# A decoder layer on one core: the output projection by seven half products for each pair of row tiles, its first products and the gate's sums inside the stage before it

## The chip, the cores and the metric

The kernel runs on one core of one Trainium2 chip. TensorE (PE) multiplies, VectorE (DVE), ScalarE (ACT) and GpSimd (POOL) work on elements, and the queue of SyncE (SP) issues nearly all transfers. The metric is the device time of one execution in microseconds (us); lower is better.

## The reference, cut to what matters

One layer with two parallel mixers (sparse attention "A", sliding-window attention "B"). The change is in what follows the attention, for 1024 positions and D = 1024:

```python
y_a = (merge_heads(o_a) * silu(z_a)) @ w_o_nsa        # (1024,512) @ (512,1024)
y_b = (merge_heads(o_b) * silu(z_b)) @ w_o_swa
m_a, m_b = split(merge)                                # columns of the input projection
y = (sigmoid(m_a) * y_a + sigmoid(m_b) * y_b) @ w_out  # (1024,1024) @ (1024,1024)
return x + gate * rms_norm(y, g_post)                  # gate = c @ w_ada[:, 2D:] + b_ada
```

## The kernel before, in words

All products are done in float32r with each operand split into a high part (a cast, on ACT) and a low part (operand minus high part, on POOL or DVE). One product of two splits is three matmuls: high by high, high by low, low by high. A matmul here takes a 128x128 block as weights and streams 512 columns.

After the attention come two stages. The **gated stage** (function `gated`) makes the gated sum `ym`, transposed (channels on partitions), in 16 steps: eight for mixer B (m = 0 to 7), then eight for mixer A. A step loads one block of `w_o` (through `wraw`, split into `wh` and `wl`, six buffers each), makes two half products of 12 matmuls (24 a step), and for each half DVE multiplies the PSUM bank by the merge gate (in `t2`, four buffers, loaded from DRAM and put through a sigmoid); in the A steps DVE also adds that to `ym` and splits `ym` into `ymh` and `yml`. Beside the B steps run `heads_out` (loads the heads' outputs `od`, splits them into `oh` and `ol`) and `w_out_block` (loads and splits `w_out`, into the places of the dead `hh` and `hl`). The **output stage** then has, for each of eight row tiles (128 positions) and each half of the columns, 24 matmuls into one bank (`out_products`), and `out_rows` makes the norm, gate and residual from the two banks and stores. Two row tiles of products are issued ahead; then `gate_rows` spreads the gate `amod` over a row by two plain float32 matmuls. The eight sums that give the gate (a multiply and reduce of 1024 elements, L1133) and their loads stand between the stages in the program.

PSUM has eight banks. `anybank` hands them out in a fixed cycle of eight, so the n-th call takes the bank of call n-8, and the matmul that starts in it waits until the readers of that one are done:

```python
order = ["s", "pt", "pj", "s", "pv", "pt", "s", "pj"]
cyc[0] += 1
return bank(order[cyc[0] % 8])
```

Each engine works its instructions in a fixed order that a scheduler sets when the kernel is built, and SP its transfers: what waits holds up all that is behind it. A tile's buffer is used again when its readers are done.

Of the kernel before, what the change touches and what calls it, by code (L numbers as in the profile page):

```python
# [14 lines left out]
P = 128  # L15
# [53 lines left out]
def hybrid_kernel(tc, io, out):  # L69
# [964 lines left out]
    with tc.tile_pool(name="ot", bufs=1, reuse_waits="tile") as op:  # L1034
        oh = [op.tile([P, S], F32R, name=f"oh{k}", tag=f"oh{k}") for k in range(8)]
        ol = [op.tile([P, S], F32R, name=f"ol{k}", tag=f"ol{k}") for k in range(8)]
        ym = {}
# [4 lines left out]
        def heads_out(k):  # L1042
            for half in range(2):
# [19 lines left out]
        for n, name in enumerate(MERGE[:KEEP]):  # L1063
            sg = op.tile([P, S], F32, name="sgm", tag=f"ym{7 - n}")
# [23 lines left out]
        woh, wol = [], []  # L1088
        ymh, yml = [], []

        def w_out_block(k):

            a, b = [], []
            for n in range(2):
                ns = slice(n * HS, n * HS + HS)
                raw = wp.tile([P, HS], F32, name="wraw", tag="wraw", bufs=3)
                nc.sync.dma_start(raw, io["w_out"][k * P : (k + 1) * P, ns])
                a.append(main.tile([P, HS], F32R, name=f"woh{k}", tag=f"hh{k}_{n}"))
                b.append(main.tile([P, HS], F32R, name=f"wol{k}", tag=f"hl{k}_{n}"))
                nc.scalar.copy(a[n], raw)  # L1100
                nc.gpsimd.tensor_tensor(b[n], raw, a[n].bitcast(F32), ALU.subtract)
            woh.append(a)
            wol.append(b)

        for m in range(8):
            ym[m] = op.tile([P, S], F32, name=f"ym{m}", tag=f"ym{m}")
            gated(m, "B", 1, lambda sl, ty, sg: nc.vector.tensor_tensor(ym[m][:, sl], ty, sg, ALU.mult))
            if m % 2:
                heads_out(m // 2)
            w_out_block(m)  # L1110
        for m in range(8):

            def emit(sl, ty, sg):
                nc.vector.tensor_tensor(sg, ty, sg, ALU.mult)
                nc.vector.tensor_tensor(ym[m][:, sl], ym[m][:, sl], sg, ALU.add)

            gated(m, "A", 0, emit)

            places = [(f"oh{m + 4}", f"ol{m + 4}")] * 4 + [("ym0", "ym1"), ("ym2", "ym3"), ("ym4", "ym5"), ("oh0", "ol0")]
            ymh.append(op.tile([P, S], F32R, name=f"ymh{m}", tag=places[m][0]))  # L1120
            yml.append(op.tile([P, S], F32R, name=f"yml{m}", tag=places[m][1]))
# [5 lines left out]
        cb2 = op.tile([P, D], F32, name="cb2", tag="ym6")  # L1127
        nc.sync.dma_start(cb2, io["c"].partition_broadcast(P))
        for k, place in enumerate(("ym7", "oh1", "ol1", "oh2", "ol2", "oh3", "ol3", "oh1")):
            blk = 16 + k  # L1130
            wa = op.tile([P, D], F32, name="wa", tag=place)
            nc.sync.dma_start(wa, io["w_adaT"][blk * P : (blk + 1) * P, :])
            nc.vector.tensor_tensor_reduce(  # L1133
                out=wa, in0=wa, in1=cb2, scale=1.0, scalar=smalls[:, 8 + blk : 9 + blk],
# [138 lines left out]
```

## Time and profile before

| what | value |
|---|---|
| time, median of 3 runs | 901.26 us (901.21 to 901.35) |
| time of the profiled execution | 900.77 us |
| its span, first to last instruction | 899.0 us |
| PE busy | 888.9 us, 99% of the span |
| DVE, ACT, POOL busy | 538.2, 505.6, 356.9 us |
| matmuls | 4538 |

The span is what the trace covers; 1.77 us of the profiled execution lie around it. A matmul's busy time includes its way through the array, so matmuls overlap and their pitch is read from their starts.

### The profile page before, as it was taken

How to read it: one execution, taken by the hardware profiler on the slowest of the kernel's cores; microseconds unless marked ns; L12 is line 12 of the kernel's file. 1: busy time of each engine (PE TensorE's matmuls, PEld its weight loads, DVE VectorE, ACT ScalarE, POOL GpSimd, SP SyncE). 2: the span in 40 equal slices, each digit the busy share in tenths (PEclk: the TensorE clock that was granted, in tenths of full speed). 3: DMA queues.
4: the chain of work that ended last, by engine and by line, in shares of the span. 5: the costliest groups of instructions: out<-in, count | busy, mean ns of one | idle time of the engine just before them, and what ended most of it. 6: DMA issues, size and time to landing. Idle time of an engine off the chain costs nothing.

```text
span 899.0 us, 14304 instructions
## 1 busy us (share of the span) xinstructions
PE 888.9 (99%) x4538; PEld 753.0 (84%) x4538; DVE 538.2 (60%) x1511; ACT 505.6 (56%) x1150; POOL 356.9 (40%) x428
## 2 busy tenths in 40 slices
PE   8999999999999999999999999999999999999997
PEld 7989888888888888888888888888887888887885
DVE  5866863465578677575585677566463372677322
ACT  6477732466676877565666777565464555442111
POOL 1000421365576866452544576453351366200000
PEclk7999999999999999999999999999999999999999
DMA  9873442342234332111222131211212677335432
GB/s 353 281 249 101 141 163 78 118 136 97 82 101 116 115 87 73 48 54 53 71 63 80 60 89 59 80 51 36 83 39 68 207 250 230 115 112 188 138 104 80
DMA packets 67087, 104.51 MB, mean 116 GB/s; under 512 B 8002, under 2 KB 25794, under 8 KB 67011
## 3 DMA queue, kind: packets, MB, share of 16 engines
q1 hardware_dynamic: 65856, 102.36, 35.1%
q10 hardware_dynamic: 1154, 1.23, 0.5%
q8 instruction: 36, 0.59, 0.3%
q14 instruction: 41, 0.33, 0.1%
HBM read 79.97 MB, written 19.92 MB: 111 GB/s over the span
## 4 chain that ended last, share of the span: by engine, by line
PE 95%; DVE 1%; DMA 1%; ACT 1%; issue 0%; POOL 0%; SPq 0%; DVEq 0%; POOLq 0%; ACTq 0%
PE b_pt L858 8%; PE b_pj L917 7%; PE b_pj L921 7%; PE b_pj L922 7%; PE b_pj L194 5%; PE b_pj L195 5%; PE b_pj L187 5%; PE b_s L790 5%; PE b_s L787 4%; PE b_pv L869 4%; PE b_pv L866 4%; PE b_s L1158 1%; PE b_s L1157 1%; PE b_s L1156 1%; PE b_s L1078 1%; PE b_s L1080 1%
## 5 line engine op out<-in xcount | busy, mean ns | idle before, releaser
L164 POOL TENSOR_TENSOR wl<-wraw,wh 128x512 fp32r<-128x512 f32 x102 | 133.7, 1313 | 137.7 <-ACT wh L161 86.6
L865 DVE TENSOR_TENSOR pl<-b_pt,ph 128x512 fp32r<-128x512 f32 x162 | 110.4, 687 | 63.2 <-ACT ph L864 62.3
L864 ACT CAST ph<-b_pt 128x512 fp32r<-128x512 f32 x162 | 93.8, 583 | 64.7 <-PE b_pt L858 51.2
L917 PE MATMUL b_pj<-hh,wh 128*128 128x512 f32 x288 | 117.6, 412 | 0.0
L922 PE MATMUL b_pj<-hh,wl 128*128 128x512 f32 x288 | 114.0, 396 | 0.0
L921 PE MATMUL b_pj<-hl,wh 128*128 128x512 f32 x288 | 113.1, 394 | 0.0
L821 POOL TENSOR_SCALAR ps<-ps,rr,gates 128x128 f32<-128x128 f32 (+7 forms) x64 | 52.7, 827 | 92.4 <-DVE rr L813 51.4
L194 PE MATMUL b_pj<-hl,wh 128*128 128x512 f32 x224 | 88.2, 394 | 0.0
L187 PE MATMUL b_pj<-hh,wh 128*128 128x512 f32 x224 | 88.0, 393 | 0.0
L195 PE MATMUL b_pj<-hh,wl 128*128 128x512 f32 x224 | 87.9, 393 | 0.0
L787 PE MATMUL b_s<-kh,q 128*128 128x256 f32 (+6 forms) x272 | 85.8, 323 | 0.0
L790 PE MATMUL b_s<-kl,q 128*128 128x256 f32 (+6 forms) x272 | 83.9, 316 | 0.0
L809 ACT ACTIVATE ps<-ps,mins 128x256 f32<-128x256 f32 (+7 forms) x96 | 64.9, 677 | 32.2 <-DVE mins L797 30.4
L161 ACT CAST wh<-wraw 128x512 fp32r<-128x512 f32 x94 | 57.5, 615 | 32.8 <-PE b_pj L194 11.7
L809 ACT ACTIVATE pw<-pw,mins 128x256 f32<-128x256 f32 (+4 forms) x96 | 60.7, 633 | 26.6 <-DVE mins L797 26.2
L869 PE MATMUL b_pv<-pl,V 128*128 128x512 f32 x162 | 67.5, 417 | 0.2
L866 PE MATMUL b_pv<-ph,V 128*128 128x512 f32 x162 | 65.3, 403 | 0.0
L922 PEld LDWEIGHTS b_pj<-hh,wl 128*128 128x128 f32 x288 | 54.1, 188 | 10.8
L921 PEld LDWEIGHTS b_pj<-hl,wh 128*128 128x128 f32 x288 | 54.4, 189 | 8.5
L880 POOL TENSOR_TENSOR ot<-ot,zt 64x512 f32<-64x512 f32 x32 | 41.2, 1288 | 49.9 <-DVE ot L879 41.0
L821 POOL TENSOR_SCALAR pw<-pw,rr,gates 128x640 f32<-128x640 f32 (+4 forms) x64 | 47.6, 748 | 32.4 <-DVE rr L813 18.0
L917 PEld LDWEIGHTS b_pj<-hh,wh 128*128 128x128 f32 x288 | 53.9, 189 | 7.5
(309 smaller groups left out, 2137.7 us busy)
## 6 DMA issues: line engine op xcount, KB each, us to landing
wraw<-in_w_blk SPq DMA_DIRECT2D x90, 256.0 KB, 2.9
wa<-in_w_adaT SPq DMA_DIRECT2D x23, 512.0 KB, 5.2
w1raw<-in_w SPq DMA_DIRECT2D x16, 256.0 KB, 3.4
od<-ot SPq DMA_DIRECT2D x64, 64.0 KB, 2.1
sp_MA<-sp SPq DMA_DIRECT2D x16, 256.0 KB, 2.0
wraw<-in_w_o SPq DMA_DIRECT2D x16, 256.0 KB, 3.4
wraw<-in_w_out SPq DMA_DIRECT2D x16, 256.0 KB, 3.7
t<-od SPq DMA_DIRECT2D x16, 256.0 KB, 4.0
```

The source lines that it names most:

```text
L164: chain("wl", nc.gpsimd.tensor_tensor(wl, raw, wh.bitcast(F32), ALU.subtract))
L187: ins = nc.tensor.matmul(t, lhsT=wh, rhs=hh[kc][half], start=(kc == 0), stop=False)
L194: nc.tensor.matmul(t, lhsT=wh, rhs=hl[kc][half], start=False, stop=False)
L195: nc.tensor.matmul(t, lhsT=wl, rhs=hh[kc][half], start=False, stop=(kc == KC - 1))
L787: ins = nc.tensor.matmul(sp[:, :n_in], lhsT=q, rhs=rh, start=True, stop=False)
L790: nc.tensor.matmul(sp[:, :n_in], lhsT=q, rhs=rl, start=False, stop=True)
L809: nc.scalar.activation(rows[r][:, :off], rows[r][:, :off], AF.Exp, scale=-1.0, bias=last_min[:, r : r + 1], accum_out=sums[:, r : r + 1])
L865: nc.vector.tensor_tensor(pl, t, ph.bitcast(F32), ALU.subtract)
L869: nc.tensor.matmul(pv, lhsT=v, rhs=pl, start=False, stop=(last and n == len(todo) - 1))
L917: ins = nc.tensor.matmul(self.t, lhsT=wh, rhs=hh[kc][self.half], start=(kc == 0), stop=False)
L921: nc.tensor.matmul(self.t, lhsT=wh, rhs=hl[kc][self.half], start=False, stop=False)
L922: ins = nc.tensor.matmul(self.t, lhsT=wl, rhs=hh[kc][self.half], start=False, stop=(kc == KC - 1))
```

## The change

The last product is done on 2 x 2 blocks. A11, A12, A21, A22 are 128 positions by 512 channels (row tiles p and p+4 of the gated sum; the second index is the half of the channels), and B11 to B22 the quarters of `w_out`. For each of four pairs p, seven products of 12 matmuls (128x512 by 512x512) take the place of eight. Their right sides are B11, B22, B21 and T1 to T4 (sums of the quarters), their left sides A11, A12, A22 and S1 to S4. The sums T are formed during the gated stage: `sums_b` in the B steps, `sums_a` in the A steps, from `w_out` rows that are loaded twice; B21 is loaded a third time (`last_set`). The sums S and the splits of the left sides (`row_set`) are made up to five products ahead. DVE adds the products up in SBUF. The gate's sums are cut into 16 of 512 elements, one in each step of the gated stage, all through one buffer (`wag`, of tag `xr`). In the list below "..." leaves out lines; T1, T2, T3, T4 are `B12-B11`, `B22-(B12-B11)`, `B22-B12` and `B21-T2`.

```diff
+        def sums_b(m):
+            k = m // 2
+            if m % 2 == 0:
+                rows[k] = w_rows(k), w_rows(k + 4)
+                r0, r1 = rows[k]
+                w_set("B11", k, r0[:, lo_], of_h(0, k))
+                nc.vector.tensor_tensor(r0[:, hi_], r0[:, hi_], r0[:, lo_], ALU.subtract)
+                w_set("T1", k, r0[:, hi_], of_h(1, k))
...
+        def sums_a(m):
...
+                r0, r1 = rows.pop(k)
+                nc.vector.tensor_tensor(r1[:, lo_], r1[:, lo_], r0[:, lo_], ALU.subtract)
+                nc.vector.tensor_tensor(r1[:, lo_], r1[:, lo_], r0[:, hi_], ALU.subtract)
+                w_set("T4", k, r1[:, lo_], of_heads(f"ol{k + 4}"))
...
+        wag = tmp("xr", 3)
+        def gate_load(k, n):
+            nc.sync.dma_start(wag, io["w_adaT"][(16 + k) * P : (17 + k) * P, n * HS : n * HS + HS])
...
-            w_out_block(m)
+            sums_b(m)
+            gate_sum(m, 0)
...
-            for half in range(2):
-                sl = slice(half * HS, half * HS + HS)
-                nc.scalar.copy(ymh[m][:, sl], ym[m][:, sl])
-                nc.vector.tensor_tensor(yml[m][:, sl], ym[m][:, sl], ymh[m][:, sl].bitcast(F32), ALU.subtract)
...
+        def split_rows(src, eng):
+            a = wp.tile([P, 4, P], F32R, name="wh", tag="wh", bufs=WBUFS)
+            b = wp.tile([P, 4, P], F32R, name="wl", tag="wl", bufs=WBUFS)
+            chain("high", nc.scalar.copy(a, src))
+            chain("vector" if eng is nc.vector else "pool", eng.tensor_tensor(b, src, a.bitcast(F32), ALU.subtract))
+            return a, b
...
+        def product(t, a, name):
+            for k in range(4):
+                bh, bl = W[name, k]
+                ins = nc.tensor.matmul(t, lhsT=a[0][:, k, :], rhs=bh, start=(k == 0), stop=False)
...
+                nc.tensor.matmul(t, lhsT=a[0][:, k, :], rhs=bl, start=False, stop=False)
+            for k in range(4):
+                nc.tensor.matmul(t, lhsT=a[1][:, k, :], rhs=W[name, k][0], start=False, stop=(k == 3))
...
+        STEPS = [("A11", "B11"), ("S3", "T3"), ("S1", "T1"), ("S2", "T2"), ("A22", "T4"), ("S4", "B22"), ("A12", "B21")]
+        todo = [(p, *f) for p in range(4) for f in STEPS]
+        todo.insert(2, todo.pop(7))
...
+            gate_load(m, 1)
+            gated(m, "A", 0, emit)
+            sums_a(m)
+            gate_sum(m, 1)
+            if m > 4:
+                sets_to(m - 4)
...
+        for step, (p, n, wn) in enumerate(todo):
+            sets_to(step + 5)
+            X, Y, V, Z = spare[p % 2]
+            t = anybank()
+            product(t, ready.pop((p, n)), wn)
+            if n == "A11":
+                nc.scalar.copy(X, t)
+            elif n in ("S3", "S1"):
+                held3[n] = t
+            elif n == "S2":
+                s3, s1 = held3.pop("S3"), held3.pop("S1")
+                nc.vector.tensor_tensor(Y, X, t, ALU.add)
+                nc.vector.tensor_tensor(Z, Y, s3, ALU.add)
+                nc.vector.tensor_tensor(V, Z, s1, ALU.add)
+                nc.vector.tensor_tensor(Y, Y, s1, ALU.add)
+            elif n == "A22":
+                nc.vector.tensor_tensor(Z, Z, t, ALU.add)
+                done_rows.append((p, [(1, V, V), (0, Z, Z)]))
+            elif n == "S4":
+                nc.vector.tensor_tensor(Y, Y, t, ALU.add)
+            elif n == "A12":
+                nc.vector.tensor_tensor(X, X, t, ALU.add)
+                done_rows.append((p + 4, [(1, Y, Y), (0, X, X)]))
+            if step == 3:
+                gate_rows()
```

The order of the products is thus A11 and S3 of pair 0, A11 of pair 1, then S1, (the two matmuls of `gate_rows`), S2, A22, S4, A12 of pair 0, S3 of pair 1 and so on.

Three places of the order that the engines work in (line numbers of the change are those of the changed kernel). The first is **POOL at the end of the gated stage**. Before, these are the last lows of `w_out` (L1101) and then only lows of `w_o` (L164), the last of them for steps A2 to A7:

```order
L1101 TENSOR_TENSOR wol6_8783<-wraw_8780,woh6_8782 128x512 [waits DMAHW5_49,Activation_49]
L164 TENSOR_TENSOR wl_8790<-wraw_8787,wh_8789 128x512 [waits DMAHW6_49,PE_49,Activation_49]
L1101 TENSOR_TENSOR wol7_8838<-wraw_8835,woh7_8837 128x512 [waits DMAHW0_49,Activation_49]
L1101 TENSOR_TENSOR wol7_8844<-wraw_8841,woh7_8843 128x512 [waits DMAHW2_49,Activation_49]
L164 TENSOR_TENSOR wl_8850<-wraw_8847,wh_8849 128x512 [waits DMAHW3_49,PE_49,Activation_49]
L164 TENSOR_TENSOR wl_8898<-wraw_8895,wh_8897 128x512 [waits DMAHW5_49,PE_49,Activation_49]
```

Now the lows of `w_o` for A6 (`wl_9166`) and A7 (`wl_9224`) stand there behind those of the first left sides (L1196: A11 of pair 0, then S3 of pair 0 from `t2_9214`); `wt` are T3 and T4:

```order
L1101 TENSOR_TENSOR wt_9154<-r_9102,wt_9154 128x512 [waits DMAHW7_49,Activation_49]
L1196 TENSOR_TENSOR wl_9159<-ym0_8395,wh_9158 128x512 [waits PE_49,Activation_49]
L164 TENSOR_TENSOR wl_9166<-wraw_9163,wh_9165 128x512 [waits PE_49,Activation_49]
L1101 TENSOR_TENSOR wt_9210<-r_9205,wt_9210 128x512 [waits DMAHW4_49,Activation_49]
L1101 TENSOR_TENSOR wt_9265<-r_9207,wt_9265 128x512 [waits DMAHW6_49,Activation_49]
L1196 TENSOR_TENSOR wl_9217<-t2_9214,wh_9216 128x512 [waits PE_49,Activation_49]
L164 TENSOR_TENSOR wl_9224<-wraw_9221,wh_9223 128x512 [waits DMAHW1_49,PE_49,Activation_49]
L1196 TENSOR_TENSOR wl_9270<-ym0_8395,wh_9269 128x512 [waits PE_49,Activation_49]
```

So two of the stage's own operands moved behind work that waits for the stage's DVE results.

The second is **DVE at the start of the output stage**. Before, it goes from the last gate sum to the rows' work, each row of which reads a bank (`b_`) as soon as it is full:

```order
L1144 TENSOR_TENSOR t_9365<-ident,amod 128x512
L1175 TENSOR_SCALAR ss<-ss 128x1
L1177 TENSOR_SCALAR rs<-ss 128x1
L1174 TENSOR_TENSOR t_9374<-b_pt,ggb 128x512
L1182 SCALAR_TENSOR_TENSOR t_9374<-t_9374,rs,xr 128x512
L1179 TENSOR_TENSOR t_9381<-b_s,ggb 128x512
```

Now sums of left sides (L1209; `t2_9390` to `t2_9599` are S3, S1, S2, S4 of pair 1 and S3, S1 of pair 2) stand ahead of the first adding up (L1304 on; `b_s_9396`, `b_s_9330`, `b_s_9367` are the products S2, S3, S1 of pair 0):

```order
L1209 TENSOR_TENSOR t2_9390<-ym0_8395 128x512 [waits DVE_49]
L1196 TENSOR_TENSOR wl_9346<-t2_9343,wh_9345 128x512 [waits PE_49,Activation_49]
L1209 TENSOR_TENSOR t2_9413<-ym0_8395,ym1_8396 128x512 [waits DVE_49]
L1209 TENSOR_TENSOR t2_9450<-t2_9413,ym0_8395 128x512 [waits DVE_49,Pool_49]
L1209 TENSOR_TENSOR t2_9505<-ym1_8396,t2_9450 128x512 [waits DVE_49,PE_49]
L1209 TENSOR_TENSOR t2_9562<-ym0_8395 128x512 [waits PE_49]
L1209 TENSOR_TENSOR t2_9599<-ym0_8395,ym1_8396 128x512 [waits Pool_49]
L1304 TENSOR_TENSOR cx_9311<-cx_9311,b_s_9396 128x512 [waits PE_49]
L1305 TENSOR_TENSOR cx_9312<-cx_9311,b_s_9330 128x512 [waits DVE_49]
```

The bank of S3 of pair 0 is read last by L1305, behind all of these.

The third is **SP where the B steps end**. Before, loads of `w_o` and of merge gates (`t2`):

```order
L1056 DMA t2_8770<-sp_MB6_4423 128x512 [waits DMAHW7_49,DVE_49]
L151 DMA wraw_8991<-in_w_o 128x512 [waits DMAHW3_49,Pool_49]
L151 DMA wraw_9039<-in_w_o 128x512 [waits DMAHW5_49,DMAHW1_49,Pool_49]
L1056 DMA t2_8806<-sp_MB7_4903 128x512 [waits DVE_49]
L151 DMA wraw_9087<-in_w_o 128x512 [waits DMAHW6_49,Pool_49]
```

Now rows of `w_out` (`r`, two buffers) and the gate's loads (`xr_8401` is `wag`) stand between them:

```order
L1105 DMA r_8898<-in_w_out 128x1024 [waits DMAHW0_49,DVE_49]
L1056 DMA t2_8814<-sp_MB7_4903 128x512 [waits DMAHW1_49,DVE_49]
L1156 DMA xr_8401<-in_w_adaT 128x512 [waits DMAHW2_49,DVE_49]
L1105 DMA r_8900<-in_w_out 128x1024 [waits DMAHW3_49,Pool_49]
L1056 DMA t2_8831<-sp_MB7_4903 128x512 [waits DMAHW4_49,DVE_49]
L151 DMA wraw_9163<-in_w_o 128x512 [waits DMAHW5_49,Pool_49]
```

Each gate load waits for the DVE sum that read the buffer before.

## Rows read from the trace of the kernel before

**Rows 1.** The page's busy times: share of the span, instructions.

```profile
span 899.0 us, 14304 instructions
PE 888.9 (99%) x4538; PEld 753.0 (84%) x4538; DVE 538.2 (60%) x1511; ACT 505.6 (56%) x1150; POOL 356.9 (40%) x428
```

**Rows 2.** The chain that ended last, in time order: start, us, engine, tile, line.

```profile
825.78 0.86 PE b_pt L1147 x2
...
827.50 0.23 PE b_s L1156
...
892.60 0.24 PE b_s L1158
892.87 0.60 ACT t L1171
```

**Rows 3.** Stretches: us, busy us of each engine, granted clock, DMA share, GB/s.

```profile
10.00:60.00 50.00, 49.37 (x239) 44.00 (x240) 38.89 (x81) 28.78 (x52) 0.00 (x0) 0.92 0.92 321
700.00:717.00 17.00, 17.00 (x76) 14.07 (x76) 6.04 (x6) 9.70 (x17) 5.58 (x4) 1.00 0.73 241
717.00:740.00 23.00, 23.00 (x103) 19.02 (x103) 17.14 (x19) 14.72 (x25) 15.88 (x12) 1.00 0.80 250
740.00:760.00 20.00, 20.00 (x90) 16.57 (x89) 4.95 (x8) 10.08 (x17) 14.53 (x12) 1.00 0.71 227
760.00:780.00 20.00, 20.00 (x90) 16.57 (x89) 10.68 (x14) 9.82 (x17) 5.67 (x5) 1.00 0.45 143
780.00:800.00 20.00, 20.00 (x89) 16.54 (x89) 14.69 (x25) 8.20 (x15) 0.00 (x0) 1.00 0.33 106
```

**Rows 4.** Matmuls in order of time: start, us; the rows shown are 27 matmuls apart.

```profile
797.74 0.39 PE L1078 MATMUL b_pj<-oh,wh 128*128 128x512 f32 x1
...
803.86 0.39 PE L1156 MATMUL b_pt<-woh,ymh 128*128 128x512 f32 x1
```

**Rows 5.** Groups by line and shape, 690 to 899: busy us, mean ns, idle before, releaser.

```profile
L1101 POOL TENSOR_TENSOR wol<-wraw,woh 128x512 fp32r<-128x512 f32 x16 | 21.3, 1339 | 20.2 <-ACT woh L1100 20.2
L1048 DVE TENSOR_TENSOR ol<-t,oh 128x512 fp32r<-128x512 f32 x16 | 18.9, 1186 | 16.8 <-ACT oh L1047 16.7
L1125 DVE TENSOR_TENSOR yml<-ym,ymh 128x512 fp32r<-128x512 f32 x16 | 11.1, 692 | 11.4 <-ACT ymh L1124 11.0
```

**Rows 6.** DVE in order of time early on: two gate-like sums of 512.

```profile
11.05 0.73 DVE L402 CUSTOM_DVE_ANT_0 wa<-wa,cb,smalls 128x512 f32<-128x512 f32 x1
11.71 0.08 DVE L402 DVE_READ_ACCUMULATOR2_ANT part<- 128x1 f32 x1
```

**Rows 7.** DVE, then POOL, in order of time around 709 us (cut by the window).

```profile
708.32 1.37 DVE L1048 TENSOR_TENSOR ol<-t,oh 128x512 fp32r<-128x512 f32 x1 [0.35 <-ACT oh L1047]
...
708.32 3.06 DVE L1048 TENSOR_TENSOR ol<-t,oh 128x512 fp32r<-128x512 f32 x2 [0.35 <-ACT oh L1047]
...
709.10 1.73 POOL L1101 TENSOR_TENSOR wol<-wraw,woh 128x512 fp32r<-128x512 f32 x1
```

**Rows 8.** The same around 740 us: POOL, then DVE reading banks.

```profile
739.59 2.55 POOL L1101 TENSOR_TENSOR wol<-wraw,woh 128x512 fp32r<-128x512 f32 x2 [1.14 <-ACT woh L1100]
...
740.12 0.67 DVE L1107 TENSOR_TENSOR ym<-b_pv,t 128x512 f32<-128x512 f32 x1
```

**Rows 9.** The loads of heads' outputs (L1046): issue to landing; SP's time for an issue.

```profile
L1046 SPq DMA_DIRECT2D t<-od x16: 319/327/543, 703.1 to 732.8; - x16
...
DMA to landing us min/median/max: 3.1/4.0/5.5
```

**Rows 10.** DVE in order of time: two adds back to back, and the last row's work.

```profile
788.94 0.68 DVE L1115 TENSOR_TENSOR ym<-ym,t 128x512 f32<-128x512 f32 x1
789.54 0.68 DVE L1114 TENSOR_TENSOR t<-b_pt,t 128x512 f32<-128x512 f32 x1
...
893.59 0.21 DVE L1177 TENSOR_SCALAR rs<-ss 128x1 f32<-128x1 f32 x1 [4.69 <-ACT t L1171]
893.72 0.68 DVE L1179 TENSOR_TENSOR t<-b_s,ggb 128x512 f32<-128x512 f32 x1
```

More of the change, by code (lines that the diff above doesn't have):

```diff
@@ L1086, in gated @@
                 emit(sl, ty, sg)
[L1088 to L1103, printed above, removed]
+        ya = [op.tile([P, 4, S], F32, name=f"ym{j}", tag=f"ym{j}") for j in range(2)]
@@ new lines, in hybrid_kernel, with gate_sum @@
+        cbs = [tmp("xr", 3) for _ in range(2)]
+        for n in range(2):
+            nc.sync.dma_start(cbs[n], io["c"][n * HS : n * HS + HS].partition_broadcast(P))
+        wag = tmp("xr", 3)
+        part = sm.tile([P, 8], F32, name="gpart")
+        def gate_load(k, n):
+            nc.sync.dma_start(wag, io["w_adaT"][(16 + k) * P : (17 + k) * P, n * HS : n * HS + HS])
+        def gate_sum(k, n):
+            blk = 16 + k
+            nc.vector.tensor_tensor_reduce(
+                out=wag, in0=wag, in1=cbs[n], scale=1.0, scalar=part[:, k : k + 1] if n else smalls[:, 8 + blk : 9 + blk],
+                op0=ALU.mult, op1=ALU.add, accum_out=mod[:, blk : blk + 1] if n else part[:, k : k + 1])
@@ L1127, in hybrid_kernel @@
[L1127 to L1134, printed above, removed]
-                op0=ALU.mult, op1=ALU.add, accum_out=mod[:, blk : blk + 1])
@@ L1136, in hybrid_kernel, with last_set @@
-        nc.vector.tensor_tensor(amod, mod[:, 16:24], g_post, ALU.mult)
-        ggb = op.tile([P, D], F32, name="ggb")
+            sums_b(m)
+            gate_sum(m, 0)
+        def last_set():
+            for k in range(4):
+                raw = wp.tile([P, HS], F32, name="wraw", tag="wraw", bufs=3)
+                nc.sync.dma_start(raw, io["w_out"][(k + 4) * P : (k + 5) * P, lo_])
+                for ins, tag in zip(w_set("B21", k, raw, of_heads(f"oh{k}")), ("high", "pool")):
+                    after(ins, last[tag])
@@ L1148, in gate_rows @@
                 nc.scalar.copy(ggb[:, n * HS : n * HS + HS], t)
-        def out_products(i):
-            sl = slice(i * P, i * P + P)
-            ts = []
-            for n in range(2):
-                t = anybank()
-                for k in range(8):
-                    nc.tensor.matmul(t, lhsT=ymh[k][:, sl], rhs=woh[k][n], start=(k == 0), stop=False)
-                    nc.tensor.matmul(t, lhsT=ymh[k][:, sl], rhs=wol[k][n], start=False, stop=False)
-                    nc.tensor.matmul(t, lhsT=yml[k][:, sl], rhs=woh[k][n], start=False, stop=(k == 7))
-                ts.append(t)
-            return ts
@@ L1162, in out_rows, with row_set, form @@
-        def out_rows(i, ts):
-            sl = slice(i * P, i * P + P)
-            xs, yg = [], []
+        def split_rows(src, eng):
[4 more added lines that the diff above has]
+            return a, b
+        sums = {}
+        def row_set(p, name):
+            down, up = slice(p * P, p * P + P), slice(HS + p * P, HS + p * P + P)
+            A = {"A11": ya[0][:, :, up], "A12": ya[1][:, :, up], "A21": ya[0][:, :, down], "A22": ya[1][:, :, down]}
+            A.update({n: sums[p, n] for n in ("S1", "S2") if (p, n) in sums})
+            def form(name, x, y, op_):
+                s = sums[p, name] = op.tile([P, 4, P], F32, name="t2", tag="t2", bufs=4)
+                nc.vector.tensor_tensor(s, A[x], A[y], op_)
+                A[name] = s
+            if name == "S3":
+                form("S3", "A11", "A21", ALU.subtract)
+            elif name == "S1":
+                form("S1", "A21", "A22", ALU.add)
+            elif name == "S2":
+                form("S2", "S1", "A11", ALU.subtract)
+            elif name == "S4":
+                form("S4", "A12", "S2", ALU.subtract)
+            return split_rows(A[name], nc.vector if p == 0 and name in ("S1", "S2", "A22", "S4") else nc.gpsimd)
@@ new lines, in hybrid_kernel @@
+        held3 = {}
+        done_rows = []
+        for step, (p, n, wn) in enumerate(todo):
[23 more added lines that the diff above has]
+                gate_rows()
+            if step > 3:
+                while done_rows:
+                    out_rows(*done_rows.pop(0))
```

105 lines of the change are left out of this document (73 added, 32 removed).

## The prediction, made before the changed kernel was run

> **What bounds the kernel now.** I read the busy times first, then the chain of waits, the stretches of the last 200 us, and the single instructions there. The reader is to see that PE is busy for 99% of the span [rows 1] and 20.00 of 20.00 us in every stretch of the gated stage, at full granted clock [rows 3], while DVE, ACT and POOL are far below that. The chain ends with the last matmul at 892.60 and the work on its bank [rows 2]. So in both stages time goes only when PE's work goes or when PE is made to wait. The pitch of a matmul is (803.86 - 797.74)/27 = 0.2267 us [rows 4]; 24 of them, a step of the gated stage, take 5.44 us. PE enters the output stage at 803.86 [rows 4] and its last matmul starts at 892.60 [rows 2].
>
> **The change part by part.** Removed: eight row tiles times two halves times 24 matmuls are 384; added: four pairs times seven products times 12 are 336. 48 matmuls at 0.2267 us are **-10.9 us** of PE. Nothing else leaves PE; the two float32 matmuls of the gate stay.
>
> The tail: before, ACT takes the last square from the bank at 892.87 [rows 2], then come a small DVE step, the last multiply [rows 10] and the store. Now DVE must first add the last bank to the sum in SBUF, an operation like L1115's or L1114's (0.68 [rows 10]), and the rest follows unchanged: **+0.7 us**.
>
> DVE, ACT and POOL beside PE. The 16 splits of `ymh` and `yml` go (0.69 us each on DVE [rows 5], and a cast on ACT), and so do the eight gate sums of 1024 that ran after the gated stage. What comes, DVE: 20 sums of `w_out` rows, 16 sums S, 16 gate sums of 512 (0.73 and 0.08 us to read the sum [rows 6]), 28 additions of banks, and its multiply by the gate now reads SBUF instead of a bank. POOL: 24 lows of `w_out` in the gated stage where there were 16, 4 more and most of the 28 left sides after it, 1.3 us each (1339 ns [rows 5]). These cost nothing while PE, at 5.44 us a step and 2.72 a product, is slower. In pure sums it is: a product needs one POOL low of 1.3 us and, over a pair of 19 us, about 23 DVE operations at the pitch of 0.60 (789.54 - 788.94 [rows 10]), some 14 us.
>
> But they are not independent. At 708.32 a DVE subtraction of two SBUF tiles takes 1.37 us instead of 0.69; POOL's instruction ends near 709.1, and the DVE one ends 0.55 us after that, at 709.69. POOL's next starts at 709.10, takes 1.73 and ends at 710.83, and DVE's second ends at 711.38 [rows 7]. They take turns: a pair costs 1.69 us (711.38 - 709.69). DVE instructions that read a bank beside a running POOL keep their 0.67 [rows 8]. That is why L1048 averages 1186 ns against 692 for L1125, which has no POOL beside it [rows 5]. The Trainium skill, "GPSIMD Engine Reference", section Key points, says that GpSimd shares its SBUF interfaces with VectorE and contends with instructions that have two SBUF inputs; these rows agree. By it the change moves work to where it collides, which the sums of the paragraph before don't see.
>
> With turns, the gated stage: from about 707 POOL has 12 lows of `w_o`, 24 of `w_out` and 2 of left sides to do, 38, before PE can begin the low part of step A7; DVE has 67 two-input SBUF instructions by then. At 1.14 and 0.55 us (as within a pair) that is 82 us, at 1.3 and 0.6 some 90 us. PE gets there about 20 matmuls before the end of the stage, near 801, after 94 us. Loads that are not there yet leave holes: DVE waited 16.8 us for the casts of these loads before [rows 5]. So between no wait and 82 to 90 plus 10 minus 94, up to 6 us. PE is protected on the bank side, seven half products (19 us) deep, so DVE's own delay shows only through the lows of A6 and A7, which now stand behind lows of left sides that wait for DVE. I take **+1.5 us** (range 0 to 6), nearer the low end, since the holes lie mostly at the start where POOL can catch up.
>
> The start of the output stage: PE does the remaining 5 matmuls of A11, then S3, A11 of pair 1, S1, the gate's two matmuls (0.86 each, 825.78 to 827.50 [rows 2]), S2, A22, S4: 77 matmuls and 1.7 us, 19.2 us after the gated stage's last matmul. The next product, A12, is the tenth call of `anybank` and takes the bank of the second, S3, read last by L1305. By then DVE must do 16 operations that stand ahead of L1304, 15 of them with two SBUF inputs, and the two adds. POOL's turns begin some 4 us in, when the first casts of B21 are done. So 0.7 + 6 x 0.6 + 9 x 1.69 + 2 x 0.6 = 20.7 us: PE waits **+1.5 us**. Without collisions 18 x 0.60 = 10.8, no wait; with every pair at 1.3 + 0.6 it is 22.6, and 3.4 us. What DVE is late by at the stage's end adds to it. After that DVE has 19 us for each pair, 12 two-input operations and 7 POOL lows (12 x 0.55 + 7 x 1.14 = 14.6) and 11 others that can run beside POOL; the left sides are five products ahead. I see no standing wait there.
>
> Transfers: before, SP moved 14.4 MB from 700 to 760 (241 GB/s for 17 us, 250 for 23, 227 for 20) at shares up to 0.80, and in the A steps only 143 and 106 GB/s [rows 3]. The change adds 8.4 MB of `w_out` rows and 4.2 MB of gate rows to the stage, and takes out 4.2 MB of `w_out`. That is about 9 MB over 100 us, 90 GB/s more; the start of the kernel held 321 GB/s at a share of 0.92 [rows 3], so it fits (about 285 on the mean), and I charge nothing beyond the wait above.
>
> Sum: -10.9 + 0.7 + 1.5 + 1.5 = -7.2 us. The span becomes 899.0 - 7.2 = 891.8, with the 1.77 us around it 893.6; the median of the runs stands 0.5 above the profiled execution, so **894.1 us**.
>
> **The rivals.**
>
> *All of it is hidden.* If the first loads arrive as early as before and POOL's work on B21 comes late enough, neither wait appears: -10.2, 891.1 us. For it: PE never waits in the present gated stage, and POOL is idle from 780 on [rows 3]. Against it: the turns of [rows 7].
>
> *The gate's loads pace the stage: slower.* The 16 gate sums go through one buffer. A turn is a sum (0.81), SP's issue (0.33 [rows 9]) and the landing, and nothing of the next can start before. With a landing of 4.0 us, the median of L1046, a turn is 5.1 us, just under the 5.44 of a step; with 5.5, the longest [rows 9], it is 6.6. The last sum stands in DVE's order at the first half of step A5, ahead of S3 of pair 0, on which the operands of A7 wait. 15 turns at 6.6 are 99 us against about 86 available from the first landing to then: 13 us late, of which some 3 are slack in A6 and A7. With SP's other waits in front of a load (a `w_out` row that waits for POOL), another 3: -7.2 + 13 = +6, about **907 us**. It decides when a turn passes 6.4 us: then the whole gain is gone. For it: more is moved, and DMA shares are 0.7 to 0.8 already in the B steps. Against: in the A steps there was room, and half of the turns lie there.
>
> *No change.* The same pacing with turns near 6.3 us, or POOL late by its bound of 6 and the bank wait by 3.4 with something of the start's loads on top: 899 to 903 us.
>
> **How the numbers follow.** Small waits as summed (892 to 897): 0.42. All hidden (890 to 892): 0.22. Waits at their bounds (897 to 899.5): 0.15. No change, within 0.2% (1.8 us), which is about what a measurement of this kernel can tell: 0.07. Slower: 0.14. So faster 0.79, same 0.07, slower 0.14. The range from 890.4 to 902.5 leaves out the slower cases and a little at the bottom; the likeliest case alone is 892 to 897.
>
> **What would show it.** Right: 336 matmuls in the output stage, PE's time in it down by 10 to 11 us but for a wait before A12 of pair 0 of 1 to 3 us whose releaser is DVE at L1305; in the gated stage waits of PE for POOL's L164 in A6 or A7 of a few us or none; DVE's L1209 and L1273 stretched above 0.69 us wherever POOL runs; the end 0.7 us longer from the last matmul. Wrong: PE waiting in the B steps; PE waiting for banks in the A steps, with DVE's L1161 waiting for DMA (the gate's loads); waits for left sides (L1195, L1196) in every pair, which would mean that DVE and POOL can't keep the pace of seven products; or a lower granted clock after such waits.

## The result and the profile after

The changed kernel took **908.89 us** (median of 4 runs, 907.19 to 909.92); the kernel before took 901.24 us (4 runs on the same chip). The ratio is 1.0088, 95% interval 1.0065 to 1.0111: slower by 7.6 us, where 894.1 was forecast, and outside the range. The profiled execution took 909.81 us; its page begins so, to be read beside [rows 1]:

```profile
span 908.0 us, 14475 instructions
...
PE 884.0 (97%) x4490; PEld 745.8 (82%) x4490; DVE 604.0 (67%) x1579; ACT 518.6 (57%) x1178; POOL 419.2 (46%) x464
```

The 48 matmuls are gone (4538 to 4490), but PE is no longer busy for 99% of the span. The view of PE's waits from 690 us to the end (engine, tile, line, releaser: us in total, times, longest) says where it stood still. Of the kernel before, the same view is empty; now it holds:

```profile
PE b_pt L1079 <- ACT wh L161: 5.8, 1, 5.8
PE b_s L1079 <- ACT wh L161: 4.6, 1, 4.6
PE b_s L1225 <- DVE cx L1304: 1.5, 1, 1.5
PE b_pt L1081 <- POOL wl L164: 1.3, 1, 1.3
```

The first, second and fourth are steps A6 and A7 waiting for their own `w_o` weights (L161 is the cast, L164 the low part); the third is the wait for a bank before A12 of pair 0. The stretches (columns as in [rows 3]) show that the waits cost more than their length, since the granted clock is lower in the stretches that hold them. From 845 to 890, in the half products, PE has no hole:

```profile
760.00:780.00 20.00, 20.00 (x90) 16.55 (x89) 12.63 (x21) 6.74 (x12) 7.06 (x5) 1.00 0.71 239
780.00:800.00 20.00, 12.90 (x54) 9.85 (x52) 15.79 (x24) 7.06 (x13) 7.69 (x6) 0.84 0.73 249
800.00:820.00 20.00, 15.39 (x47) 11.98 (x48) 13.87 (x23) 5.36 (x10) 8.05 (x5) 0.73 0.42 132
845.00:890.00 45.00, 45.00 (x200) 37.28 (x199) 40.17 (x56) 16.89 (x40) 26.38 (x21) 1.00 0.35 115
```

PE in order of time at A6, where the start of each row matters more than its length:

```profile
791.29 0.39 PE L1081 MATMUL b_s<-oh,wl 128*128 128x512 f32 x1
797.50 0.79 PE L1079 MATMUL b_pt<-oh,wh 128*128 128x512 f32 x1 [5.81 <-ACT wh L161]
798.09 0.63 PE L1080 MATMUL b_pt<-ol,wh 128*128 128x512 f32 x1
800.00 0.80 PE L1081 MATMUL b_pt<-oh,wl 128*128 128x512 f32 x1 [1.29 <-POOL wl L164]
800.60 0.63 PE L1079 MATMUL b_pt<-oh,wh 128*128 128x512 f32 x1
801.02 0.63 PE L1080 MATMUL b_pt<-ol,wh 128*128 128x512 f32 x1
...
803.99 0.39 PE L1081 MATMUL b_pt<-oh,wl 128*128 128x512 f32 x1
804.22 0.39 PE L1079 MATMUL b_pj<-oh,wh 128*128 128x512 f32 x1
```

After the wait the pitch is 0.43 us (800.60 to 801.02), and from 803.99 on 0.23 again: half speed, 1.2 instead of 2.4 GHz. The same happens from 812.20 to 817.77, after the wait of A7.

**Where the time went.** From the first gated matmul (715.01; 716.82 before) to the start of the last one (899.33, the last of the four in a row that begins at 898.65; 892.44 before) PE took 184.3 us instead of 175.6, 8.7 more. The last matmul of the kernel before, in PE's order of time:

```profile
892.44 0.39 PE L1158 MATMUL b_s<-woh,yml 128*128 128x512 f32 x1
```

([rows 2] have 892.60 for it: a row of that chain begins where the one before it ended, here at 892.21 + 0.39, and not at the start of the instruction.) Removed matmuls give -10.9. The pauses beyond the pitch are 5.98 and 1.68 in A6, 4.76 in A7 and 1.65 before A12, **+14.1**. Half speed after the waits is 2.3 and 2.6, **+4.9**. That makes +8.1; the other 0.6 is spread over gaps too short to follow. The tail from the last matmul's start is 8.7 us (908.0 - 899.33) against 6.6 (899.0 - 892.44), **+2.1**. The part before the gated stage was 1.8 us shorter in this execution. Together 9.0, the difference of the spans (908.0 - 899.0).

**Why the weights of A6 and A7 come late.** ACT, in order of time, before either of them:

```profile
795.79 0.63 ACT L1057 ACTIVATE t<-t 128x512 f32<-128x512 f32 x1 [3.81 <-DMA t<-sp_MA]
796.32 0.60 ACT L1195 CAST wh<-ym 128x512 fp32r<-128x512 f32 x1
796.83 0.61 ACT L161 CAST wh<-wraw 128x512 fp32r<-128x512 f32 x1
...
811.01 0.62 ACT L1195 CAST wh<-t 128x512 fp32r<-128x512 f32 x1 [0.19 <-DVE amod L1281]
811.53 0.61 ACT L161 CAST wh<-wraw 128x512 fp32r<-128x512 f32 x1
```

The cast that PE needs (L161) stands on ACT behind a cast of a left side (L1195), as its low part does on POOL in the order shown before the run, and behind a sigmoid of a merge gate (L1057). The left side waits for DVE, and DVE is late; the merge gate's load is late too, as SP's rows below show. At A6 ACT stood 3.81 us for that load, and the left side was ready by then; at A7 the left side came 0.19 us later than the sigmoid was through. DVE in order of time; between these rows it does the stage's other work:

```profile
775.63 0.69 DVE L1141 TENSOR_TENSOR r<-r 128x512 f32<-128x512 f32 x1 [2.99 <-DMA r<-in_w_out]
777.44 1.79 DVE L1161 CUSTOM_DVE_ANT_0 xr<-xr,gpart 128x512 f32<-128x512 f32 x1
787.67 0.69 DVE L1141 TENSOR_TENSOR r<-r 128x512 f32<-128x512 f32 x1 [1.54 <-DMA r<-in_w_out]
798.10 0.72 DVE L1141 TENSOR_TENSOR r<-r 128x512 f32<-128x512 f32 x1 [2.29 <-DMA r<-in_w_out]
809.53 0.75 DVE L1161 CUSTOM_DVE_ANT_0 xr<-xr,gpart 128x512 f32<-128x512 f32 x1 [1.55 <-DMA xr<-in_w_adaT]
810.21 0.69 DVE L1209 TENSOR_TENSOR t<-ym 128x512 f32<-128x512 f32 x1
```

The last row forms S3, whose cast at 811.01 holds up A7's. It stands directly behind the last gate sum (L1161), which waited for its load. SP, in order of time, with the loads of the gate (L1156) and of the `w_out` rows (L1105):

```profile
779.26 0.33 SPq L1156 DMA_DIRECT2D xr<-in_w_adaT  x1
...
780.51 0.33 SPq L1105 DMA_DIRECT2D r<-in_w_out  x1
...
791.96 0.33 SPq L1056 DMA_DIRECT2D t<-sp_MA  x1
```

The gate load at 779.26 could not be issued before the sum of 777.44 had read the one buffer (it ended at 779.2), and the next `w_out` rows stand behind it on SP. DVE then waits for those rows (787.67, 798.10), with the next gate sum behind them, which frees the buffer late. So the two loads hold each other up through two in-order queues, and the merge gates' loads stand between them on SP: the last row is the one that ACT waited for at A6, issued behind a gate load (789.66) and `w_out` rows (791.40) that had both waited for DVE. The waits of DVE, then of SP's queue, from 700 to 845 us (in total, times, longest):

```profile
DVE xr L1161 <- DMA xr<-in_w_adaT: 11.2, 7, 3.5
...
DVE r L1141 <- DMA r<-in_w_out: 6.8, 3, 3.0
```

```profile
SPq L1156 <- DVE mod L1161: 19.4, 7, 6.2
...
SPq L1156 <- DVE gpart L1161: 7.9, 6, 3.2
```

The 16 sums start from 710.99 to 809.53: 15 turns of 6.57 us on the mean, though a landing took 4.0 us at the median, as [rows 9] had it. SP lost nothing: in 14 of the 15 turns it issued the load 0.04 us after the sum that freed the buffer. But the sum itself took 1.3 us on the mean instead of 0.75, and it stood 1.2 us on the mean behind other work of DVE after its load had landed (the 13 turns in which the trace tells the landing). The view of the buffer's tile (durations in ns min/median/max, first and last start):

```profile
L1161 DVE CUSTOM_DVE_ANT_0 xr<-xr,smalls x8: 735/1777/1854, 711.0 to 765.6; 128x512 f32<-128x512 f32 x8
L1161 DVE CUSTOM_DVE_ANT_0 xr<-xr,gpart x8: 747/1084/1787, 770.5 to 809.5; 128x512 f32<-128x512 f32 x8
...
DMA to landing us min/median/max: 2.6/4.0/7.0
```

All this is a reading of one trace. The theory is that **the gate's one buffer makes DVE late in the stage**. Its rivals: the place of the left sides ahead of A6's and A7's casts; the amount moved (`w_out` rows); the work of the gate's sums wherever they stand; VectorE's load beside GpSimd in the half products.

### The profile page after: what moved, and what is told of

Read it like the earlier page. It is cut to its first block, busy times and chain, and to the rows that moved or that the text cites. A ratio compares the mean times of both kernels' runs of the same rounds, so it can differ in the third digit from the quotient of the medians.

```text
span 908.0 us, 14475 instructions
## 1 busy us (share of the span) xinstructions
PE 884.0 (97%) x4490; PEld 745.8 (82%) x4490; DVE 604.0 (67%) x1579; ACT 518.6 (57%) x1178; POOL 419.2 (46%) x464
## 4 chain that ended last, share of the span: by engine, by line
PE 80%; DMA 6%; DVE 6%; issue 3%; ACT 2%; POOL 2%; SPq 0%; DVEq 0%; POOLq 0%; ACTq 0%
PE b_pt L858 8%; PE b_pj L917 7%; PE b_pj L921 7%; PE b_pj L922 7%; PE b_pj L194 5%; PE b_pj L195 5%; PE b_pj L187 5%; PE b_s L790 5%; PE b_s L787 4%; PE b_pv L869 4%; PE b_pv L866 4%; DMA r<-in_w_out 3%; DMA xr<-in_w_adaT 1%; PE b_s L210 1%; PE b_s L211 1%
## 5 line engine op out<-in xcount | busy, mean ns | idle before, releaser
L164 POOL TENSOR_TENSOR wl<-wraw,wh 128x512 fp32r<-128x512 f32 x102 | 136.8, 1344 | 128.1 <-ACT wh L161 80.0
L161 ACT CAST wh<-wraw 128x512 fp32r<-128x512 f32 x94 | 57.4, 614 | 31.8 <-PE b_pj L194 15.1
```

What stands on the lines that cost most here:

```text
L164: chain("wl", nc.gpsimd.tensor_tensor(wl, raw, wh.bitcast(F32), ALU.subtract))
```

## Experiments

Each was compared with the kernel before on its own chip. Edits are against the changed kernel unless another is named. The ratios, for reading across:

| kernel | us | ratio to before (95%) |
|---|---|---|
| changed kernel | 908.89 | 1.0088 (1.0065 to 1.0111) |
| 1 no gate | 901.45 | 1.0010 (1.0000 to 1.0019) |
| 2 weights of A6, A7 first | 907.83 | 1.0087 (1.0068 to 1.0106) |
| 3 `w_out` rows loaded once | 905.52 | 1.0060 (1.0039 to 1.0081) |
| 4 before, gate moved alone | 911.58 | 1.0116 (1.0098 to 1.0135) |
| 5 gate behind the stage, weights first | 898.87 | 0.9981 (0.9969 to 0.9993) |
| 6 three gate buffers, weights first | 898.10 | 0.9975 (0.9966 to 0.9985) |
| 7 no left sides in the stage | 906.04 | 1.0066 (1.0044 to 1.0087) |
| 8 half the gate behind the stage | 899.04 | 0.9984 (0.9971 to 0.9996) |
| 9 three gate buffers alone | 902.60 | 1.0026 (1.0016 to 1.0037) |
| 10 as 6, gate's rows later | 901.11 | 1.0010 (0.9997 to 1.0023) |
| 11 as 4, three gate buffers | 902.92 | 1.0039 (1.0027 to 1.0051) |
| 12 as 6, gate's diagonals on ACT | 897.03 | 0.9971 (0.9961 to 0.9982) |

### First round: which part of the change is slow

**1, no gate** (the gate's loads and sums are left out; its rows come from the bias alone).

```diff
         def gate_load(k, n):
+            return
...
         def gate_sum(k, n):
+            return
...
-        nc.vector.tensor_tensor(amod, mod[:, 16:24], g_post, ALU.mult)
+        nc.vector.tensor_tensor(amod, b_gt, g_post, ALU.mult)
```

> Leaves out the gate's loads and its 16 sums (the gate is the bias alone), everything else as in the change. If the gate's one buffer, with SP and DVE waiting for each other through it, paces the gated stage: PE's two long waits in A6 and A7 (5.8 and 4.6 us) and the half clock behind them go, and the time falls by 12 to 16 us to 893 to 897. If the rows of w_out or the order on ACT are to blame instead: the waits stay within a third, 904 us or more.

Measured 901.45, between the two cases: 0.78% below the changed kernel's ratio, some 7 us. So the gate is most of the loss and not all of it; PE still waited 2.7 us for A6's cast and 2.0 us for its low part. DVE waited 15.1 us for `w_out` rows here (700 to 845), more than twice the 6.8 of the changed kernel, so DVE's waits can't simply be added up to PE's loss.

**2, weights first** (the loads and casts of the weights of A6 and A7 stand ahead of the left sides).

```diff
+        def load_wo(side, m):
+            if m < 8 and (side, m) not in wos:
+                wos[side, m] = load_half(io["w_o"][side, m])
...
             if m > 4:
+                load_wo(0, m + 1)
                 sets_to(m - 4)
```

> The load and split of w_o for steps A6 and A7 stand in the program ahead of the first left sides. If DVE's lateness reaches PE only through the order on ACT and POOL (casts of w_o behind casts that wait for DVE): the waits in A6 and A7 go, but DVE stays late, so PE waits at the first left sides or the first bank of the output stage instead: 898 to 905 us. If the order is not the way in which it reaches PE: no change, 907 to 910.

907.83, no gain (1.0087): the waits moved as in the first case, the time is the second's. The waits at A6 and A7 nearly went (one of 1.5 and one of 1.3 us are left), and others came: 4.4 us at the matmuls of the gate's rows, which wait for DVE, and 2.8 us for left sides. DVE is late whatever PE asks of it next, so here the order only says where PE pays.

**3, rows once** (the A steps form T3 and T4 from the first step's rows, without six loads of 512 KB).

```diff
-                rows[k] = w_rows(k), w_rows(k + 4)
+                rows[k] = (w_rows(k), w_rows(k + 4)) if k == 0 else held_rows
+                held_rows[:] = rows[k]
```

> In the A steps the rows of w_out are loaded once and not four times (T3 and T4 come from the wrong rows for three of four blocks): six loads of 512 KB less, all sums and splits kept. If the rows' landing (up to 6.7 us, DVE waiting at L1141) is what makes DVE late: the waits in A6 and A7 go, 893 to 898 us. If the gate's buffer is enough by itself to make it late: 903 us or more.

905.52, the second case. PE's wait at A6 was 8.9 us in one piece. DVE waited for rows no longer than 1.3 us at any place from 740 to 815, but 9.3 us for gate loads. So the `w_out` rows are at most a small part (2.5 us by the ratios, whose intervals overlap), and the gate's loads make DVE late without them.

**4, the gate alone** (the kernel before, with its gate sums replaced by the changed kernel's 16 in the stage; the last product as before).

```diff
+            gate_load(m, 1)
             gated(m, "A", 0, emit)
...
+            gate_sum(m, 1)
```

> The kernel before, with only the gate's sums moved into the gated stage (16 halves through one buffer) and the old output products. If the gate's buffer alone paces the stage: PE waits in the A steps, 904 to 912 us. If it takes gate and rows of w_out together (my reading: DVE waits for rows, the gate's sum stands behind, SP waits for the sum and issues the next rows late): the turn of 5.1 us stays under a step's 5.44 and the time is that of before, 900 to 902.5.

911.58, 10.7 us more than before, with no half product in it: the first case, and against my reading of the trace, which wanted the `w_out` rows too. That is more than the whole change costs. DVE's waits from 740 to 815, then PE's from 690 on:

```profile
DVE xr L1117 <- DMA xr<-in_w_adaT: 21.2, 9, 4.4
```

```profile
PE b_pt L1167 <- ACT ymh L1143: 7.8, 3, 3.8
```

Its turns took only 5.11 us (sums from 710.96 to 787.64), shorter than a step of 5.44 and the very number of the prediction. Yet DVE, which works in order, waited for a load in nine of them, seven times for 1.8 to 4.4 us, while multiplications stood ready behind. One of them, then the multiplications of the B steps (L1124) and of the A steps (L1132) by DVE between the fifth sum and the last (us, busy us, in brackets how many):

```profile
758.90 1.84 DVE L1117 CUSTOM_DVE_ANT_0 xr<-xr,gpart 128x512 f32<-128x512 f32 x1 [4.42 <-DMA xr<-in_w_adaT]
```

```profile
738.80:787.60 48.80, 7.33 (x11) 1.00 0.66 219
```

```profile
738.80:787.60 48.80, 2.74 (x4) 1.00 0.66 219
```

These are 15 half products, which PE makes in 15 x 2.72 = 40.8 us, and 11 turns, which took 48.8: DVE fell behind by 8 us. The reason lies in the order of instructions. The program has one sum in each step, but in DVE's fixed order all 16 stand ahead of the 21st of the 32 multiplications, so that eleven come in seven and a half steps, and a turn that is shorter than a step is still too long.

After the last sum (787.64) DVE did not catch up: PE waited for `ymh` three times, until 818.08. ACT's waits from 740 to 820 show what held DVE then:

```profile
ACT t L1057 <- DMA t<-sp_MA: 24.3, 15, 2.5
```

A merge gate's load goes into one of four buffers that DVE must have read, so a late DVE also makes these loads late. From 793.73 to 809.18 DVE multiplied six banks, one every 2.6 us, against the 2.72 in which PE fills one: the lateness hardly shrank.

### Second round: the buffer, the order, or the work

**5, the gate behind the stage** (all 16 loads and sums after the last A step, in three buffers that are free there; gate's rows at the eighth product; weights first as in 2).

```diff
-            gate_load(m, 1)
...
-            gate_sum(m, 1)
...
+        for k in range(8):
+            for n in range(2):
+                gate_load(k, n)
+                gate_sum(k, n)
...
-            if step == 3:
+            if step == 7:
```

> All 16 gate sums and their loads stand behind the gated stage, in three buffers, inside the first seven products of the last product; gate's rows and the output rows start at the eighth product instead of the fourth; the weights of A6 and A7 are loaded ahead of the first left sides. Nothing is left out. If the lost time comes from DVE waiting for gate loads in the stage plus the place of the left sides, both go: no TensorE wait above 1.5 us before 845 us, and 893 to 897 us. If the 16 sums cost the same wherever they stand beside the left sides (DVE is the bound), TensorE waits for wl or wh inside the first two pairs and the time is 901 to 906 us.

898.87, between the two cases. The execution that was traced took 3128 us, the nine others 896.56 to 900.50, so that no wait is read from it.

**6, three buffers and weights first** (the gate stays in the stage; its loads of the A steps take the three buffers of `t1`, which the heads' loads no longer need there).

```diff
+        wag_b = tmp("xr", 3)
+        wags = {}
...
         def gate_load(k, n):
+            wag = wags[k, n] = tmp("t1", 3) if n else wag_b
```

> The gate's sums stay in the stage; in the A steps their loads go through three buffers instead of one; the weights of A6 and A7 are loaded ahead of the first left sides. Nothing is left out. If the one buffer (a load can't be issued before the sum ahead of it is done) is what makes DVE late, DVE's waits for xr of 11 us go and the time is 895 to 899 us. If the loads themselves, or DVE's and ACT's work, are what is late, the waits move to the w_out rows or to t and the time stays at 903 to 908 us.

898.10, the first case. Against 2, whose program differs in the buffers alone, the ratio falls from 1.0087 to 0.9975, about 10 us. DVE's waits for gate loads are 3.0 and 1.1 us, and the last sum starts at 775.2 instead of 809.53. It also stands elsewhere in DVE's fixed order, which is set anew for each kernel: ahead of it are 18 of the 32 multiplications by a merge gate, and 27 in the changed kernel. What the buffers give and what this place gives was not told apart. No wait is left at A6 or A7. What is left in PE's waits is the start of the half products:

```profile
PE b_pt L1199 <- DVE t L1196: 4.4, 1, 4.4
```

**7, no left sides in the stage** (one buffer, as in the changed kernel).

```diff
-            if m > 4:
-                sets_to(m - 4)
```

> The gate's sums stay in the stage through one buffer, but no left side is formed inside it: all six first ones stand behind the last A step. Nothing is left out. If the left sides ahead of the casts of the weights cause the waits of A6 and A7, TensorE's waits for wh go and come back smaller at the start of the last product: 897 to 901 us. If the gate's lateness is enough by itself, as in the kernel that moved the gate alone, 904 to 908 us.

906.04, the second case. The waits at A6 and A7 went, and one of 9.9 us came at S3, the second half product, for a left side's cast. Moving the left sides moves the wait.

**8, half the gate behind the stage** (the B steps' eight sums stay, the A steps' eight stand behind it; weights first; gate's rows and output rows at the sixth product; row tile 3's last scaling held until the last sum is out).

```diff
-            gate_load(m, 1)
...
+                for o in end_rows if p == 3 else []:
+                    after(o, ins)
...
-            if step == 3:
+            if step == 5:
```

> Half of the gate's sums (those of the B steps) stay in the stage, the eight of the A steps stand behind it in three buffers; the weights of A6 and A7 are loaded ahead of the first left sides; row tile 3's last scaling waits until the last product's sum is out. Nothing is left out. If the A steps' gate and the order are the cause, the stage runs without a wait above 1.5 us, the tail is about 1 us shorter than the changed kernel's 8.4 us, and the time is 891 to 895 us. If B steps' sums already make the stage late, 897 us or more.

899.04. The stage ran without a wait, as in the first case, but the time is the second's (897 or more): the gate's rows came late (2.4 and 2.2 us on DVE). The tail did not get shorter by 1 us: the last sum began 0.4 us after the last matmul's start instead of 1.4, but row tile 3's scaling then stood ahead of the last `rs`. From the last matmul to the end it took 8.1 us, against 8.7.

### Third round: one edit at a time

**9, three buffers alone**: the edit of 6 without the weights first.

> The changed kernel with one thing different: the gate's loads of the A steps go through three buffers instead of one. Nothing is left out. If the one buffer is the cause and the place of the left sides is a matter of a few us only, the waits of A6 and A7 for wh shrink to those of the kernel without a gate (about 3 and 2 us) and the time is 899 to 903 us. If both are needed, waits of 4 us and more stay at A6 and A7 and the time is 904 to 908 us.

902.60, as the first case had it. The ratio falls from 1.0088 to 1.0026, about 5.6 us, by the buffers alone. PE's waits at A6 and A7, to be compared with the four of the changed kernel:

```profile
PE b_pt L1079 <- ACT wh L161: 2.4, 1, 2.4
...
PE b_s L1081 <- POOL wl L164: 1.3, 1, 1.3
PE b_pt L1081 <- POOL wl L164: 1.3, 1, 1.3
PE b_s L1079 <- ACT wh L161: 0.8, 1, 0.8
```

From here to 6 (0.9975) is the weights' place, some 4.6 us. The same edit gained nothing in 2: in these runs it counts only once DVE is on time.

**10, gate's rows later** (6, with the gate's rows and the first output rows at the eighth product).

```diff
-            if step == 3:
+            if step == 7:
```

> Three buffers for the gate's loads of the A steps, the weights of A6 and A7 ahead of the first left sides, and the gate's rows and the first output rows four products later (at the eighth product). Nothing is left out. If the wait for the gate's rows (4.4 us with the same two edits and rows at the fourth product) is only a matter of their place, it goes, with the half clock behind it: 891 to 894 us. If DVE has no room in the first pair, the wait comes back at a left side's low part or a bank: 896 to 899 us.

901.11, above both cases. The wait of 4.4 us went; one of 3.2 us came at the gate's rows for a bank that DVE had not read, and the output rows, begun later, made the end longer: the profiled execution ran 11.7 us on from the last matmul's start (885.5 to 897.2). Asking DVE later did not help.

**11, the gate alone with three buffers** (4, with the loads of the A steps in three buffers).

```diff
+            wag = wags[k, n] = tmp("t1", 3) if n else wag_b
```

> The kernel before with the gate's sums moved into the stage, as in the run that moved the gate alone, but with three buffers for the loads of the A steps. Last product as before, nothing left out. If the one buffer was the whole of that run's loss of 10.7 us, 899 to 902 us. If the gate's loads or sums cost the stage by themselves, 906 us or more.

902.92, between the two cases; the ratio falls from 1.0116 to 1.0039, about 7 us. The buffer is most of that run's loss. The rest, 3.5 us, is not: PE waited 1.9 us in the stage, and the last matmul starts at 895.17 against 892.44.

**12, the diagonals on ACT** (6, with the two diagonal tiles for the gate's rows made by ACT).

```diff
-                nc.vector.tensor_tensor(
-                    dg.rearrange("p (k t) -> p k t", k=4), ident.unsqueeze(1).broadcast_to([P, 4, P]),
-                    amod[:, 4 * n : 4 * n + 4].unsqueeze(2).broadcast_to([P, 4, P]), ALU.mult)
+                for k in range(4):
+                    nc.scalar.activation(dg[:, k * P : k * P + P], ident, AF.Copy, scale=amod[:, 4 * n + k : 4 * n + k + 1])
```

> Three buffers for the gate's loads of the A steps, the weights of A6 and A7 ahead of the first left sides, and the diagonal tiles for the gate's rows formed by ScalarE in eight pieces of 128x128 instead of by VectorE in two of 128x512. Nothing is left out. With the first two edits alone TensorE waited 4.4 us at the gate's rows, behind 3.4 us of VectorE for these tiles and 6.9 us of low parts and sums ahead of them, and ran at half clock after it; that kernel took 898.1 us. If VectorE's work at the start of the last product is what is left, the wait falls below 2 us and the time is 893 to 896 us. If the wait returns elsewhere as with the rows four products later, 897 to 900 us.

897.03 (9 runs), ratio 0.9971: faster than both kernels, by 2.6 us against before. Against 6 (0.9975) that is 0.4 us, with intervals that overlap: the gain of 2 to 5 us did not come, and the second case holds. The wait at the gate's rows fell to 1.0 us, and one for a bank came:

```profile
PE b_s L1234 <- DVE cx L1314: 2.6, 1, 2.6
PE b_pt L1198 <- ACT t L1197: 1.0, 1, 1.0
```

A likely reason why it stops here is seen in the stretch from 800 to 890 us, of the kernel before, then of this one:

```profile
800.00:890.00 90.00, 90.00 (x395) 73.82 (x394) 40.78 (x76) 15.65 (x39) 3.86 (x7) 1.00 0.40 135
```

```profile
800.00:890.00 90.00, 82.32 (x355) 65.96 (x353) 81.86 (x107) 36.51 (x82) 50.49 (x37) 1.00 0.26 87
```

DVE is busy for 81.86 of 90 us where it was busy for 40.78, and POOL for 50.49 instead of 3.86; PE's waits above are for DVE and ACT. The half products save PE 10.9 us and bring DVE to nine tenths of its time. Part of that is DVE standing beside POOL (a subtraction took 0.69 us or up to 1.8 at the start of the changed kernel's output stage), which no run took away.

## Why the prediction was wrong

**The step that failed** is the last one of the sum, on transfers: "so it fits, and I charge nothing beyond the wait above". Bandwidth did fit: the A steps moved 239 and 249 GB/s. What did not fit was the turn of the gate's one buffer, put at 5.1 us in the forecast case. It measured 6.57, with the landing as assumed (4.0 at the median, 7.0 at most): the sum took 1.3 us instead of 0.81, and it stood 1.2 us behind other work of DVE. The one buffer costs about 5.6 us in the changed kernel (9), 10 us with the weights first (6 against 2) and 7 us without any half product (11 against 4).

**The rival named it.** "The gate's loads pace the stage" gave about 907 us and 908.89 was measured; a chance of 0.14 was too little for it. Its bound of 6.4 us for a turn was passed, and its 15 turns, 99 us, measured 98.5. That is partly luck: it reached 6.6 by a landing of 5.5, where the sum and DVE's other work made the turn long. It counted rightly up to the last sum's place at A5; what misled was to hold the turn against the 5.44 of a step as well, as run 4 shows with turns of 5.11 and a loss of 10.7.

**A second step failed beside it.** The forecast is 0.992 of the kernel before and 1.0088 was measured, about 15 us apart. The buffers give back 5.6 (9) and the weights' place another 4.6 (6); some 5 stay in 6. There PE waits 4.4 us for the gate's rows. The forecast let the gate's two matmuls run without a wait: it counted DVE's work at the start of the output stage only against the bank of A12, not against these matmuls, which come three products earlier.

**A6 and A7.** The wait of 1.5 us (range 0 to 6) was 12.4 us in pauses. The place was right (L161 and L164 behind the casts and lows of left sides that wait for DVE), the cause was put on POOL's turns instead of on late loads that DVE and ACT wait for. The chain of operands was seen in the order of instructions; that DVE would be late was not. (The forecast's 38 x 1.14 + 67 x 0.55 is 80 and not 82 us, which changes no bound.)

**The clock** was named as a sign at the end and was no term. Rows show 4.9 us of it here.

**The tail** was +0.7 and is +2.1. The last addition begins 1.4 us after the last matmul's start, since row tile 3's scaling and a multiply stand ahead of it on DVE. DVE in order of time:

```profile
898.73 1.41 DVE L1252 SCALAR_TENSOR_TENSOR cx<-cx,rs,xr 128x512 f32<-128x512 f32 x2
900.06 0.69 DVE L1244 TENSOR_TENSOR cx<-cx,ggb 128x512 f32<-128x512 f32 x1
...
900.73 0.68 DVE L1314 TENSOR_TENSOR cx<-cx,b_pj 128x512 f32<-128x512 f32 x1
```

Run 8 took that delay away and got back 0.6 us of the tail. By the rows of the trace the addition is 0.7 of the 2.1, as forecast, this delay 1.0, and 0.4 lie between the start of the last square and that of the last scaling (2.0 us against 1.7).

**What held.** 48 matmuls are gone at the forecast pitch. The bank wait before A12 of pair 0 was put at 1.5 and is 1.5, with DVE at L1304 as the releaser, one line ahead of the L1305 that was named. The number is partly luck: one addition fewer was waited for, and DVE stood 1.2 us for a buffer that POOL was reading, which was no term:

```profile
834.72 1.76 DVE L1209 TENSOR_TENSOR t<-t,ym 128x512 f32<-128x512 f32 x1 [1.19 <-POOL wl L1196]
```

After it PE had no hole from 845 to 890, as forecast.

**Left open.** Run 11's last 3.5 us are only partly named, and how much of what is left in 6 and 9 is DVE and POOL taking turns was not measured by itself, and no run sets three buffers apart from the order that comes with them. The Trainium skill, "Trainium Kernel Development and Optimization", section Best Practices, advises to double-buffer so that transfers overlap with compute; runs 9 and 11 agree: three buffers for eight of the 16 loads of 256 KB gave back 5.6 and 7 us.

## What to carry to other kernels

Before a load through one buffer is called free, look up the order that the engine which reads it will work in, and count how much of the busiest engine's work stands between one read and the next; it need not be one step, though the program says so (run 4 had eleven reads in seven and a half steps). Hold that against a turn made of the landing, the read as it runs in that place (1.3 us here, where 0.75 is the least) and what the reading engine does in between. A share of bandwidth does not answer the question. When work is moved into a stage that runs without a hole, look at what each in-order engine must finish at the end of the stage, and test the cover by giving the moved loads more buffers before touching the order; the order gained nothing here until the lateness was gone, and 4.6 us after. Saving matmuls with additions pays only as far as the adding engine has time: here 10.9 us saved on TensorE gave 2.6 at best, with VectorE at nine tenths.

## What the runs showed of the hardware

After pauses of 6.0 and 4.8 us TensorE went on at a pitch of 0.43 us instead of 0.23, from 797.50 to 803.99 and from 812.20 to 817.77, with a mean granted clock of 0.84 and 0.73 in those stretches of 20 us; 2.3 and 2.6 us were lost so, on top of the pauses. A gate sum of 512 columns, 0.73 us in [rows 6], took from 0.73 to 1.85 us in the gated stage. In the changed kernel the long ones (1.4 us and more) began while a GpSimd subtraction of 128x512 ran and ended some 0.55 us after it: the sum of 777.44 at 779.23, the GpSimd instruction beside it at 778.67:

```profile
777.05 1.62 POOL L1101 TENSOR_TENSOR wt<-r,wt 128x512 fp32r<-128x512 f32 x1 [7.01 <-ACT wt L1101]
```
